# A decoder layer on one core: squares of the next group's input further behind their loads, priority for masked values and for heads' second parts, the last group's first two output blocks stored singly

## The chip, the cores and the metric

The kernel runs on one core of a Trainium2 chip. A core has four compute engines that run their own instruction streams, TensorE (PE, matrix products, with its weight load PEld beside it), VectorE (DVE), ScalarE (ACT) and GpSimd (POOL), and SyncE (SP), which here issues nearly all of the transfers (DMA) between the chip's memory and the core's own. The streams wait for each other by semaphores. The metric is the device time of one launch in microseconds (us); smaller is better.

## The reference

One layer of a decoder, in fp32, for a prompt of 2048 tokens and for 8 samples of 8 tokens that share the weights (model width 1024):

```python
hp = rmsnorm(x, norm_mix_w)
proj = hp @ w_in                       # 8 parts of 4 heads x 128
rq, rk, rv, rg, hq, hf, hi, hg = split(proj)
# 4 RetNet heads: rotary q and k, decay 1 - 2^(-5-h), state S <- g*S + k^T v, o = q S
# 4 HGRN2 heads: f = lb + (1-lb)*sigmoid(hf), state S <- diag(f) S + (1-f)^T hi, o = silu(hq) S
o = head_rmsnorm(o) * silu(gate)       # per head
x = x + concat(o) @ w_out
x = x + square(relu(rmsnorm(x) @ w_up)) @ w_down
y = rmsnorm(x)                         # and the heads' final states, of prompt and samples
```

## The kernel before, in words

**Numbers and tiles.** Tokens lie in the free dimension, 128 features in the partitions. A product of fp32 operands is made from "first parts" (`hi`, rounded to fp32r by a copy) and "second parts" (`lo`, the remainder, one subtraction): hi*hi, hi*lo and lo*hi, three matmuls into one PSUM tile. For weights, `hi` is L311 on ACT and `lo` L318 on DVE; for the groups' input the pair is L1961 (ACT) and L1965 (DVE), named `first` and `second` of `halve`, and "cut" in `operands`. The larger products are made from quarters of their operands in seven products instead of eight, which needs sums of quarters: L429 and L1901 for weights (kept in the chip's memory for later groups: L436 stores the sums, L400 the first and second parts), L879 (`total`) for the input.

**The work in stages.** The tokens come in three groups: group 0 has the 64 sample tokens and 512 of the prompt (T = 576), groups 1 and 2 have 768 each. For each group `mix` goes through four head pairs (p = 0 to 3): it projects queries, keys and gates (products L464 in group 0, L1125 and L1868 later), the values (L1202, L1206 in group 0), and runs the chunks of the retention and of the gated recurrence: scores L1482, turns of keys L1393, states and outputs L1707, L1709, L1715, samples L1324, L1327, L1378. The heads' outputs go to memory (L1241) until the group's heads are complete, are loaded back (L1236), transposed on PE and cut (`cut_heads`, L1857 to L1859). `out_proj` projects them in 8 blocks, in two loops in group 0: the first three heads' part first, evicted onto the residual, then the last head's. Then the MLP runs for the group, and the next group begins.

**Early operands.** While group 0's last head and output projection run, group 1's input is already read and prepared by `norm_blocks` with `early`: `operands` loads four quarters of x (`load`, L1941 on SP), squares them for the RMSNorm (`square`: L854 on ACT, the sum L856 on DVE), multiplies them by the norm's weight (`weigh`, L863 on ACT, two instructions each), cuts them, and makes the sums L879 and cuts these. It does so for v = 0 and for v = 1; the squares' sum then goes through L2038, L682, L683 and PE's column sums L688 and L689 to the factor of the norm. Group 2's input is prepared in the same way during group 1's MLP, without squares.

**What sets the order.** The program is written along PE's steps. `later(ticks, fn)` puts a step on an agenda so many ticks (steps of PE's products) ahead, and it is emitted when that tick comes. The instructions so emitted get their place on each engine from a scheduler, which estimates when each is ready; `soon` (L246) emits an instruction with high priority, and an instruction so emitted is listed under L246 in a profile, whatever it does; `keep_in_program_order` pins it against others so marked. DMA issues have a place in SP's or ACT's order like any instruction, so a transfer that waits holds up those behind it.

**The places that the change touches.** `sample_blocks` (L1366) multiplies a value tile by the samples' mask for `sample_update` (L1378 on PE, L1382 and L1385 on DVE). `cut_heads` makes the first part of the transposed heads on ACT and the second on DVE:

```python
self.tc.keep_in_program_order(nc.scalar.activation(hi[:, a:e], ps, AF.Copy, scale=w))
nc.vector.scalar_tensor_tensor(out=lo[:, a:e], in0=ps, scalar=w, in1=hi.bitcast(F32)[:, a:e], ...
```

`finish_last` ends the program: the last group's column sums (L2427 on PE), the norm's factor (L2358 and L2359 on ACT), eight multiplies L2436 of 128 partitions x 384 on DVE, each half of the columns of a pair of blocks, and four stores L2437, one for each pair (`np_` 0 to 3), alternately issued by SP and ACT.

## Time and profile before

| | |
|---|---|
| median of 3 runs | 2358.68 us (2358.43 to 2358.98) |
| the profiled execution | 2359.45 us |
| its span (first to last instruction) | 2357.6 us |
| PE busy | 2337.3 us (99%) |
| DVE busy | 1792.8 us (76%) |
| ACT busy | 1227.3 us (52%) |
| POOL busy | 139.1 us (6%) |
| chain of work that ended last | PE 93%, DVE 3%, ACT 1%, DMA 1%, issue 1% |
| moved by DMA | 575.60 MB, mean 244 GB/s |

Busy is the time in which an engine works on an instruction; issuing transfers and waiting on semaphores are not counted. The chain is followed back from the last instruction, at each step to what released it. Profile rows of several instructions give their count as x4; the releaser in brackets ("0.72 <-ACT slab L246") is the idle time before the row and what ended it. Names without numbers (slab, ld, raw, pj, mm) are pools of buffers: slab and ld are 128 x 768 tiles, ld those that transfers fill; pj and mm lie in PSUM, which PE writes.

### The profile page before, as it was taken

What the parts mean: (1) busy time and instruction counts of PE and PEld (TensorE: products, weight loads), DVE (VectorE), ACT (ScalarE), POOL (GpSimd) and SP (SyncE); (2) the same over time, 40 slices, a digit from 0 to 9 for tenths busy, and PEclk for the clock granted to TensorE, in tenths of its full rate; (3) what the DMA queues carried; (4) which work ended last, traced back from release to release, by engine and by line L of the source; (5) the groups of instructions that cost most, each with busy time, mean ns of one, the idle gap of its engine ahead of it and who ended that gap; (6) DMA issues with size and microseconds to landing.
All of it is one profiled execution on the core that took longest, in us unless ns stands there. A gap on an engine that the chain in (4) does not pass through costs nothing.

```text
span 2357.6 us, 39360 instructions
## 1 busy us (share of the span) xinstructions
PE 2337.3 (99%) x15340; PEld 2301.6 (98%) x15340; DVE 1792.8 (76%) x2309; ACT 1227.3 (52%) x1976; POOL 139.1 (6%) x199
## 2 busy tenths in 40 slices
PE   9999999999999999999999999999999999999998
PEld 8888899999999999999999999999999999999997
DVE  8766766777666776668769988666988787669887
ACT  5556555557645555546455546444544364445443
POOL 3221201111001100100000000000000000000000
PEclk9999999999999999999999999999999999999999
DMA  9888887779866777898677665767665458675642
GB/s 317 285 296 298 267 314 255 280 266 324 302 226 242 273 285 286 300 344 304 219 258 262 219 219 189 248 206 229 224 194 186 152 192 270 194 232 179 207 154 70
DMA packets 232649, 575.60 MB, mean 244 GB/s; under 512 B 24195, under 2 KB 92803, under 8 KB 232454
## 3 DMA queue, kind: packets, MB, share of 16 engines
q1 hardware_dynamic: 231766, 572.20, 71.3%
q8 instruction: 122, 2.00, 0.4%
q10 hardware_dynamic: 688, 0.80, 0.1%
q14 instruction: 73, 0.60, 0.1%
HBM read 419.95 MB, written 151.66 MB: 242 GB/s over the span
## 4 chain that ended last, share of the span: by engine, by line
PE 93%; DVE 3%; ACT 1%; DMA 1%; issue 1%; POOL 0%; SPq 0%; DVEq 0%; POOLq 0%; ACTq 0%
PE pj L1868 36%; PE pf L1868 28%; PE pj L464 11%; PE pj L1125 10%; PE pj L1206 2%; PE mm L1707 1%; PE mm L1715 1%; PE mm L1709 1%; PE mm L1393 1%; PE mm L1482 1%; PE mm L1635 1%; PE mm L1206 0%; PE mm L1857 0%; DVE raw L429 0%; DVE lo L318 0%
## 5 line engine op out<-in xcount | busy, mean ns | idle before, releaser
L1868 PE MATMUL pj<-slab,hi 128*128 128x384 f32 (+1 forms) x3504 | 853.4, 326 | 0.0
L311 ACT CAST hi<-raw 128x1024 fp32r<-128x1024 f32 x446 | 468.6, 1051 | 692.1 <-PE pj L1868 264.6
L318 DVE TENSOR_TENSOR lo<-raw,hi 128x1024 fp32r<-128x1024 f32 x446 | 545.8, 1224 | 157.3 <-ACT hi L311 152.2
L1868 PE MATMUL pf<-slab,hi 128*128 128x384 f32 (+1 forms) x2768 | 652.2, 321 | 0.0
L1868 PEld LDWEIGHTS pj<-slab,hi 128*128 128x128 f32 x3504 | 614.3, 188 | 0.0
L1868 PE MATMUL pj<-slab,lo 128*128 128x384 f32 (+1 forms) x1752 | 570.7, 326 | 0.0
L1868 PEld LDWEIGHTS pf<-slab,hi 128*128 128x128 f32 x2768 | 480.0, 188 | 0.1
L1868 PE MATMUL pf<-slab,lo 128*128 128x384 f32 (+1 forms) x1384 | 443.1, 320 | 0.0
L1868 PEld LDWEIGHTS pj<-slab,lo 128*128 128x128 f32 x1752 | 329.3, 188 | 0.0
L1125 PE MATMUL pj<-hi,slab 128*128 128x256 f32 x1344 | 260.4, 287 | 0.3 <-DVE slab L246 0.3
L1868 PEld LDWEIGHTS pf<-slab,lo 128*128 128x128 f32 x1384 | 260.1, 188 | 0.0
L464 PE MATMUL pj<-slab,hi 128*128 128x288 f32 (+1 forms) x1216 | 243.4, 316 | 2.1 <-ACT slab L246 1.0
L1125 PEld LDWEIGHTS pj<-hi,slab 128*128 128x128 f32 x1344 | 214.9, 191 | 0.6 <-DVE slab L246 0.6
L464 PEld LDWEIGHTS pj<-slab,hi 128*128 128x128 f32 x1216 | 194.2, 188 | 5.3 <-issue 1.8
L1125 PE MATMUL pj<-lo,slab 128*128 128x256 f32 x672 | 190.1, 283 | 0.0
L1961 ACT CAST slab<-slab 128x768 fp32r<-128x768 f32 (+1 forms) x192 | 145.4, 779 | 62.9 <-DVE slab L1972 47.4
L246 DVE TENSOR_TENSOR slab<-pj,slab 128x768 f32<-128x768 f32 (+2 forms) x136 | 124.2, 915 | 70.4 <-PE pj L1868 27.3
L1965 DVE TENSOR_TENSOR slab<-slab 128x768 fp32r<-128x768 f32 (+1 forms) x192 | 167.3, 886 | 13.2 <-ACT slab L1961 4.6
L464 PE MATMUL pj<-slab,lo 128*128 128x288 f32 (+1 forms) x608 | 143.5, 315 | 0.0
L1125 PEld LDWEIGHTS pj<-lo,slab 128*128 128x128 f32 x672 | 128.7, 192 | 0.0
L464 PEld LDWEIGHTS pj<-slab,lo 128*128 128x128 f32 x608 | 102.6, 188 | 0.3 <-issue 0.2
L2217 DVE TENSOR_TENSOR slab<-pf,slab 128x768 f32<-128x768 f32 (+1 forms) x87 | 76.5, 884 | 24.4 <-PE pf L1868 24.2
(265 smaller groups left out, 2572.0 us busy)
## 6 DMA issues: line engine op xcount, KB each, us to landing
raw<-w SPq DMA_DIRECT2D x254, 512.0 KB, 5.2
slab<-fu SPq DMA_DIRECT2D x64, 384.0 KB, 5.3
fu<-ld SPq DMA_DIRECT2D x60, 384.0 KB, 3.9
ld<-fin SPq DMA_DIRECT2D x28, 384.0 KB, 5.0
ld<-x SPq DMA_DIRECT2D x24, 384.0 KB, 7.0
slab<-fu SPq DMA_DIRECT2D x32, 288.0 KB, 4.8
fu<-ld SPq DMA_DIRECT2D x30, 288.0 KB, 3.2
slab<-x SPq DMA_DIRECT2D x16, 384.0 KB, 6.7
```

The source lines that it names most:

```text
L246: return fn(*a, **k)
L311: self.nc.scalar.copy(self.wts[j][0], raw)
L318: self.nc.vector.tensor_tensor(out=lo, in0=raw, in1=hi.bitcast(F32), op=ALU.subtract)
L464: self.nc.tensor.matmul(pj[:, i, :T2], w, a[:, c0:c1], start=j == 0 and q == 0, stop=j == n - 1 and q == 2)
L1125: self.nc.tensor.matmul(ps[:, tb * 256:(tb + 1) * 256], t, w[:, cols], start=first and kb == j == 0 and tb != 1, stop=kb == KB // 2 - 1 an ...
L1206: nc.tensor.matmul(dst, t[:, s:s + C], ww, start=kb == 0 and q == 0, stop=last and q == 2, skip_group_check=True)
L1393: nc.tensor.transpose(ps[:, j * P:(j + 1) * P], src[:, c], self.ident)
L1482: nc.tensor.matmul(ps[:, j * P:(j + 1) * P], k[:, cols[c]], q[:, cols[c]], start=True, stop=True)
L1868: m = self.nc.tensor.matmul(*a, **k)
L1961: self.nc.scalar.copy(hi[:, :g.T], B[name][:, :g.T])
L1965: self.nc.vector.tensor_tensor(out=lo[:, :g.T], in0=B[name][:, :g.T], in1=hi.bitcast(F32)[:, :g.T], op=ALU.subtract)
L2217: nc.vector.tensor_tensor(out=r, in0=ps, in1=r, op=ALU.add)
```

## The change

It alters the ticks of three calls and of three steps in `operands`, the priority of two DVE instructions, and the end:

- group 1's early operands: v = 0 loads from tick 40 instead of 44 and sums from 92 instead of 88; v = 1 from 96 and 148 instead of 100 and 144;
- in `operands`, each quarter's square comes 22 ticks behind its load instead of 9, its weighing 24 instead of 12 (20 where there are no squares), its cut 30 instead of 18 (26);
- the masked values and the heads' second parts are emitted with `soon`;
- of the last group's four output pairs the first is multiplied block by block (four multiplies of 128 x 192, in program order) and stored as two blocks, one by SP and one by ACT; the other three pairs stay pairs, and go to SP, ACT, SP where they went to ACT, SP, ACT.

```diff
--- before.py
+++ after.py
@@ -830,7 +830,7 @@
 
         if early:
             x.update(split=split, factor=factor, factor_t=factor_t)
-            self.operands(g, 0, 44, 88, x, 186)
+            self.operands(g, 0, 40, 92, x, 186)
             return
         todo = [(m, v, h) for h in range(2) for m in range(2) for v in range(2)]
         for k, a in enumerate(todo):
@@ -870,10 +870,10 @@
             t = t0 + 7 * j
             self.later(t, load, name)
             if sums is not None:
-                self.later(t + 9, square, name)
-            self.later(t + (12 if sums is not None else 20), weigh, name)
+                self.later(t + 22, square, name)
+            self.later(t + 24, weigh, name)
             if name != "B12":
-                cut(t + (18 if sums is not None else 26), name)
+                cut(t + 30, name)
         def total(name, into):
             a, op, b = T_SUMS[name]
             nc.vector.tensor_tensor(out=B[into][:, :g.T], in0=B[a][:, :g.T], in1=B[b][:, :g.T], op=op)
@@ -904,7 +904,7 @@
             self.later(164, tables)
             self.later(176, rotary)
             return
-        self.operands(g, 1, 100, 144, g.x)
+        self.operands(g, 1, 96, 148, g.x)
         for h in range(2):
             self.later(146 + 4 * h, g.x["split"], h)
             self.later(154 + 4 * h, g.x["factor"], h)
@@ -1363,7 +1363,7 @@
         for i in range(2):
             vm = self.getr()
             v = w[i].bitcast(F32)[:96, which * P:(which + 1) * P]
-            self.nc.vector.tensor_tensor(out=vm[:96, :512].rearrange("p (s v) -> p s v", v=P),
+            self.soon(self.nc.vector.tensor_tensor, out=vm[:96, :512].rearrange("p (s v) -> p s v", v=P),
                                          in0=v.unsqueeze(1).to_broadcast([96, 4, P]),
                                          in1=self.con[:96, C_SM:C_SM + 4].unsqueeze(2).to_broadcast([96, 4, P]), op=ALU.mult)
             out.append(vm)
@@ -1856,8 +1856,8 @@
                     c = (j - j0) * 256 + hd * P
                     nc.tensor.transpose(ps[:, s:s + n], o[:n, c:c + P], self.ident[:n, :n])
                 self.tc.keep_in_program_order(nc.scalar.activation(hi[:, a:e], ps, AF.Copy, scale=w))
-                nc.vector.scalar_tensor_tensor(out=lo[:, a:e], in0=ps, scalar=w, in1=hi.bitcast(F32)[:, a:e],
-                                               op0=ALU.mult, op1=ALU.subtract)
+                self.soon(nc.vector.scalar_tensor_tensor, out=lo[:, a:e], in0=ps, scalar=w, in1=hi.bitcast(F32)[:, a:e],
+                          op0=ALU.mult, op1=ALU.subtract)
             g.oc[p].append((hi, lo))
 
     def pair(self, g, slab):
@@ -2430,11 +2430,18 @@
             t = self.get()
             for ps, c in zip(x["ps"], two):
                 self.soon(self.last_factor, ps, t[:, c])
-            for np_ in range(4):
+            y = self.outputs(g, 0)
+            for c in two:
+                for i in range(2):
+                    r = block(i)[:, c]
+                    self.tc.keep_in_program_order(nc.vector.tensor_tensor(out=r, in0=r, in1=t[:, c], op=ALU.mult))
+            for i, queue in enumerate((nc.sync, nc.scalar)):
+                queue.dma_start(y[:, i], block(i))
+            for np_ in range(1, 4):
                 r = self.pair(g, g.R[np_ % 2][np_ // 2, 0])
                 for c in two:
                     nc.vector.tensor_tensor(out=r[:, :, c], in0=r[:, :, c], in1=t[:, c].unsqueeze(1).to_broadcast([P, 2, w // 2]), op=ALU.mult)
-                (nc.scalar if np_ % 2 else nc.sync).dma_start(self.outputs(g, 0)[:, 2 * np_:2 * np_ + 2], r)
+                (nc.sync if np_ % 2 else nc.scalar).dma_start(y[:, 2 * np_:2 * np_ + 2], r)
 
         for d, fn, *a in ((13, squares), (14, weigh, 0), (15, weigh, 1), (17, total), (19, square, 2), (20, third), (21, weigh, 2),
                           (25, square, 3), (26, lambda: sums(x["sum"], True)), (27, weigh, 3), (29, lambda: sums(x[3], False)), (30, outs)):
```

How this moves instructions is seen in three places. All rows are in the order in which the engine runs them; a row of several equal instructions has their count behind it.

The first place is group 0's last head. On DVE, from the first sum of squares on, there stood before:

```order
L856 TENSOR_TENSOR slab<-slab 128x768
L1965 TENSOR_TENSOR slab<-ld,slab 128x768
L246 TENSOR_TENSOR slab<-pj,ld 128x576
L1755 SCALAR_TENSOR_TENSOR slab<-mm,rs,slab 128x128 x2
L1965 TENSOR_TENSOR slab<-ld,slab 128x768
L1755 SCALAR_TENSOR_TENSOR slab<-mm,rs,slab 128x128 x2
L856 TENSOR_TENSOR slab<-slab 128x768
L1965 TENSOR_TENSOR slab<-ld,slab 128x768
L1022 TENSOR_TENSOR slab<-slab 128x576
L318 TENSOR_TENSOR lo<-raw,hi 128x1024
```

and now:

```order
L856 TENSOR_TENSOR slab<-slab 128x768
L246 TENSOR_TENSOR slab<-pj,ld 128x576
L1755 SCALAR_TENSOR_TENSOR slab<-mm,rs,slab 128x128 x4
L1965 TENSOR_TENSOR slab<-ld,slab 128x768
L1022 TENSOR_TENSOR slab<-slab 128x576
L318 TENSOR_TENSOR lo<-raw,hi 128x1024
L1965 TENSOR_TENSOR slab<-ld,slab 128x768
L318 TENSOR_TENSOR lo<-raw,hi 128x1024
```

The second part of the value weights (L318) has two cuts and the second sum of squares less ahead of it. On SP, a little later, the heads' results (fo) are loaded back; before:

```order
L1241 DMA fo_2851<-slab 128x512
L252 DMA raw<-w 128x1024 x3
L1236 DMA ld<-fo_1336 128x768
L1236 DMA ld<-fo_1338 128x512
L1236 DMA ld<-fo_2068 128x768
L1236 DMA ld<-fo_2070 128x512
L436 DMA fsi3VS_2898<-raw 128x2x256
L1236 DMA ld<-fo_2849 128x768
L436 DMA fsi3VS_2905<-raw 128x2x256
```

and now:

```order
L1241 DMA fo_2847<-slab 128x512
L252 DMA raw<-w 128x1024 x2
L436 DMA fsi3VS_2898<-raw 128x2x256
L436 DMA fsi3VS_2905<-raw 128x2x256
L400 DMA fki3VA11hi<-hi 128x2x256
L1236 DMA ld<-fo_1336 128x768
L1236 DMA ld<-fo_1338 128x512
L400 DMA fki3VA11lo<-lo 128x2x256
L252 DMA raw<-w 128x1024
L1236 DMA ld<-fo_2068 128x768
L1236 DMA ld<-fo_2070 128x512
```

Three stores of 256 KB stand ahead of the first load now, and a store and a weight load of 512 KB between the first two loads and the next two.

The second place is the end of the same head's values on PE, with the turns L1393 of its keys. pj tiles are numbered as allocated; mm_3057 and mm_3084 are the turns' tiles. Before:

```order
L1206 MATMUL pj_2799<-hi_2878,slab_176 128x512
L1206 MATMUL pj_2799<-lo_2879,slab_176 128x512
L1206 MATMUL pj_2799<-hi_2878,slab_177 128x512
L1206 MATMUL pj_2799<-hi_2878,slab_184 128x512
L1206 MATMUL pj_2799<-lo_2879,slab_184 128x512
L1393 MATMUL mm_3057<-con_78,slab_2413 128x128 x2
L1206 MATMUL pj_2799<-hi_2878,slab_185 128x512
L1627 MATMUL mm_3062<-slab_2711,slab_2795 128x64
L1393 MATMUL mm_3084<-con_78,slab_2413 128x128 x2
L1206 MATMUL pj_2798<-hi_2878,slab_176 128x512
```

and now:

```order
L1206 MATMUL pj_2797<-hi_2878,slab_176 128x512
L1393 MATMUL mm_3057<-con_78,slab_2413 128x128 x2
L1206 MATMUL pj_2797<-lo_2879,slab_176 128x512
L1206 MATMUL pj_2797<-hi_2878,slab_177 128x512
L1627 MATMUL mm_3062<-slab_2703,slab_2793 128x64
L1393 MATMUL mm_3084<-con_78,slab_2413 128x128 x2
L1206 MATMUL pj_2797<-hi_2878,slab_184 128x512
L1206 MATMUL pj_2797<-lo_2879,slab_184 128x512
L1206 MATMUL pj_2797<-hi_2878,slab_185 128x512
L1206 MATMUL pj_2796<-hi_2878,slab_176 128x512
```

Both turns stand three or four products earlier.

The third place is the output projection of group 0 on DVE, where the first loop's last block is evicted (from pj_3715, block 8) and the second loop's first (from pj_3786, in the new order pj_3775). Before:

```order
L2038 TENSOR_TENSOR slab_2597<-slab_2597 128x384
L1965 TENSOR_TENSOR slab_3747<-ld_3691,slab_3746 128x768
L246 TENSOR_TENSOR slab_3265<-pj_3786,slab_3265 128x576
L246 TENSOR_TENSOR slab_3778<-pj_3715,slab_3713 128x576
L856 TENSOR_TENSOR slab_2685<-slab_2685,slab_3764 128x768
```

and now:

```order
L2038 TENSOR_TENSOR slab_2652<-slab_2652 128x384
L246 TENSOR_TENSOR slab_3767<-pj_3715,slab_3713 128x576
L1965 TENSOR_TENSOR slab_3765<-ld_3683,slab_3764 128x768
L246 TENSOR_TENSOR slab_3265<-pj_3775,slab_3265 128x576
L856 TENSOR_TENSOR slab_2724<-slab_2724,slab_3791 128x768
```

Block 8's eviction now stands ahead of the cut and of the next block's eviction.

## Rows read from the trace of the kernel before

**Rows 1.** The page: busy time of PE, its share of the span, its instructions.

```profile
PE 2337.3 (99%) x15340; PEld 2301.6 (98%) x15340; DVE 1792.8 (76%) x2309; ACT 1227.3 (52%) x1976; POOL 139.1 (6%) x199
```

**Rows 2.** Windows of 50 us: length, each engine's busy us, clock, DMA share, GB/s.

```profile
200.00:250.00 50.00, 47.78 (x318) 41.70 (x314) 42.44 (x71) 33.95 (x76) 15.36 (x16) 1.00 0.80 269
250.00:300.00 50.00, 47.57 (x348) 42.27 (x348) 35.55 (x69) 29.72 (x78) 6.89 (x11) 1.00 0.91 303
300.00:350.00 50.00, 49.15 (x335) 48.85 (x335) 35.93 (x45) 31.99 (x48) 1.93 (x3) 1.00 0.87 309
...
550.00:600.00 50.00, 48.77 (x349) 47.24 (x348) 44.83 (x73) 33.43 (x71) 7.04 (x9) 1.00 0.87 299
```

**Rows 3.** Waits of PE: us in total, times, longest.

```profile
PE mm L1709 <- ACT slab L246: 1.1, 1, 1.1
...
PE pj L464 <- ACT slab L246: 1.0, 1, 1.0
PE pj L464 <- DVE slab L246: 0.9, 1, 0.9
PE pj L1202 <- DVE lo L318: 0.8, 1, 0.8
PE mm L1378 <- DVE slab L1366: 0.7, 1, 0.7
PE pj L1206 <- ACT slab L246: 0.7, 1, 0.7
PE mm L1857 <- DVE slab L1859: 0.5, 1, 0.5
```

**Rows 4.** Timeline of PE, 233 to 235 us: start, length, instruction, idle before.

```profile
233.19 0.39 PE L1202 MATMUL pj<-hi,slab 128*128 128x512 f32 x1
233.42 0.39 PE L1206 MATMUL mm<-hi,slab 128*128 128x512 f32 x1
234.65 0.50 PE L1202 MATMUL pj<-lo,slab 128*128 128x512 f32 x1 [0.85 <-DVE lo L318]
```

**Rows 5.** Timeline of ACT, 219 to 221 us.

```profile
219.74 0.84 ACT L854 ACTIVATE slab<-ld 128x768 f32<-128x768 f32 x1 [1.53 <-DMA ld<-x]
220.49 0.39 ACT L246 ACTIVATE slab<-S,G 128x128 f32<-128x128 f32 x1
```

**Rows 6.** Timeline of DVE, 230 to 233 us.

```profile
230.96 0.96 DVE L856 TENSOR_TENSOR slab<-slab 128x768 f32<-128x768 f32 x1
231.84 0.95 DVE L1965 TENSOR_TENSOR slab<-ld,slab 128x768 fp32r<-128x768 f32 x1
```

**Rows 7.** Timelines of POOL, SP (issues) and PE, 237 to 245 us.

```profile
237.72 2.77 POOL L1021 TENSOR_TENSOR slab<-slab,ld 128x576 f32<-128x576 f32 x1 [8.20 <-ACT slab L246]
...
240.52 0.80 SPq L1236 DMA_DIRECT2D ld<-fo  x2
...
244.40 0.86 PE L1857 MATMUL mm<-con,ld 64*128 64x64 f32 x5
```

**Rows 8.** Lines L1021 (all), L1236 issued at 241.0, L1236 (all): ns; us to landing.

```profile
L1021 POOL TENSOR_TENSOR slab<-slab,ld x8: 1429/1442/2772, 32.2 to 237.7; 128x576 f32<-128x576 f32 x8
...
DMA to landing us min/median/max: 3.2/3.2/3.2
...
DMA to landing us min/median/max: 2.8/4.4/9.2
```

**Rows 9.** Timeline of ACT, 259 to 264 us.

```profile
259.33 0.37 ACT L1395 COPY slab<-mm 128x256 f32<-128x256 f32 x1 [1.14 <-PE mm L1393]
...
262.88 1.05 ACT L311 CAST hi<-raw 128x1024 fp32r<-128x1024 f32 x1 [1.20 <-DMA fki3VA22hi<-hi]
```

**Rows 10.** Timeline of DVE, 316 to 320 us.

```profile
318.78 1.42 DVE L246 TENSOR_TENSOR slab<-pj,slab 128x576 f32<-128x576 f32 x2 [1.90 <-PE pj L464]
```

**Rows 11.** Timeline of DVE, 2346 to 2352 us.

```profile
2346.80 3.84 DVE L2436 TENSOR_TENSOR slab<-slab 128x384 f32<-128x384 f32 x8 [0.72 <-ACT slab L2359]
```

**Rows 12.** Line L2437, the last stores: us from issue to landing.

```profile
DMA to landing us min/median/max: 3.6/5.2/5.2
```

## The prediction

> **What bounds the kernel now.** Read the engines' busy times first: TensorE (PE) works 2337.3 us of a 2357.6 us span, 99% [rows 1]. A change that adds no arithmetic can therefore pay only where PE stands idle. The table of 50 us stretches shows where that is: PE has 47.78, 47.57 and 49.15 us of 50 in the three stretches from 200 to 350 us, and 48.77 from 550 to 600 [rows 2]: 6.7 us are missing in these four together. The list of PE's waits then says for whom it stood idle [rows 3]: six of the seven entries lie between 219 and 320 us, that is in the last head (p = 3) of the first group and in its output projection, where the change moves squares, loads and second parts. The seven make 5.7 us; the start and the tail have what else PE lacks. A wait costs PE a restart on top: after the 0.8 us for L1202 the matmul starts 1.23 us after the one before, where two neighbours stand 0.23 apart [rows 4], 1.0 in all. I count 0.2 for each restart.
>
> The sum is made against the profiled execution, 2359.45 us (its span of 2357.6 and 1.85 around it); it lies 0.77 above the median of 2358.68. 0.2%, about what a measurement of this kernel can tell from no change, is 4.7 us.
>
> **The parts, in the order of time.**
>
> *First square (PE waits at 219.4).* PE waits 1.1 us for ScalarE's (ACT's) next state, L246 [rows 3]. ACT stood idle 1.53 us for a load of x, squared it for 0.84 us, and only then reached L246 at 220.49 [rows 5]. Moving the squares 13 ticks behind their loads is just what should remove this. But in the new order the first L854 still stands ahead of that L246, and the loads' issue stands at the same place on SP, behind the two stores of the samples' states. So I take 0. Bounds: a gain of 1.3, the whole wait with its restart, or a loss of 1.5, ACT's idle time once more, if the load lands that much later now that a second one follows it at once on SP.
>
> *Second part of the value weights (PE waits at 233.4).* PE waits 0.8 us for L318 on VectorE (DVE) [rows 3]. An L856 at 230.96 and an L1965 at 231.84, of the squares and the cuts, stood ahead of it [rows 6]. Both now stand behind it: L318 starts twice 0.88 us earlier, and the wait goes, 1.0 us with its restart.
>
> *But the next wait is close.* PE comes to the heads' first transposes (L1857) at 244.40, without a wait [rows 7]. They read head results that SP loads back at L1236, first issued at 240.52, when GpSimd (POOL) ends its L1021 (237.72 plus 2.77) and with it the last use of the buffer; the second load lands 3.2 us after its issue at about 241.0 [rows 7, 8], so at 244.2. PE would now come 1.0 us earlier, and by the new order the transposes stand three products (0.7 us) sooner: it would be there at 242.7. ACT's copy that starts L1021 keeps its time in the new order, because it stands behind a cut that needs a DVE sum. So most of the 1.0 is waited away again. Net gain between 1.0 (loads earlier) and -0.5 (three stores of 256 KB now go out ahead of them): I take 0.4.
>
> L1021's own length decides here: seven of the eight took about 1.44 us, this one 2.77, beside DVE operations that read two SBUF tensors [rows 8]. The Trainium skill, "SBUF — State Buffer", section "Who interferes with whom", says that a DVE instruction with two SBUF inputs and a GpSimd instruction that reads SBUF exclude each other, and whichever issues second waits until the first is done. The long row agrees with it, and DVE still has such instructions at that time in the new order, so by that rule the length is a matter of which came first.
>
> *Masked values and second parts of the heads get priority.* PE waited 0.7 us for L1366 at 282.5 [rows 3]; there the order of DVE is unchanged (two L965, L1382, L1965 still ahead): 0. For heads 1 and 2 it does change, but their masked values are not among PE's waits: 0. The heads' second parts (L1859) now go ahead of the weight sums L429 around 249 us; of what PE lacks from 200 to 250 [rows 2] the named waits leave 0.3, so this gives between 0 and 0.3, and I take 0.2.
>
> *Evictions of the last values (PE waits at 259.9).* PE waits 0.7 us for ACT's L246 [rows 3]; ACT had itself been idle 1.14 us for the turn L1393, until 259.33 [rows 9]. In the new order that turn stands four products earlier, so the evictions can run beside them. Gain 0 (if the turn's PSUM buffer is not free sooner) to 0.9 with the restart: 0.6.
>
> *First out-projection blocks (PE waits at 263.5).* PE waits 1.0 us for L246 on ACT [rows 3], which stands behind an L311 that waited 1.20 us, until 262.88, for the store of kept weights fki3VA22hi [rows 9]. That store stood on SP behind stores of weight sums; three of the sums (L429) now come ahead of an L246 and the scans L1437 on DVE, and SP is past them sooner. Gain 0 to 1.2: 0.8.
>
> *The eighth block (PE waits at 318.5).* PE waits 0.9 us for DVE [rows 3]: DVE, idle 1.90 us for PE, first evicts block 1 of the second loop and then block 8 of the first [rows 10], so the next block finds no free buffer. In the new order block 8 comes three places earlier, ahead of an L1965, in that idle time. Gain 1.1, or 0 if block 8's x, whose load now stands one transfer later on SP, is not there yet; DVE's idle time leaves 1.9 us for that: 0.8.
>
> *Group 1's first head (590 us).* PE waits 0.5 us for L1859 [rows 3], and again for the L246 behind it. Now all four L1859 go ahead of L246, and all twelve transposes ahead of the products. The fourth L1859 lengthens L246's wait by about 0.5 us, of which the three transposes that PE does meanwhile fill 0.3: a loss of 0.2 (0 to 0.5). The same swap in group 2's head and group 2's later sums lie in stretches without a gap: 0.
>
> *The end.* Eight multiplies take 3.84 us together, 0.48 each [rows 11]; two of them become four halves. Halves cost between half and all of a whole, so the last store goes 0 to 0.96 us later; I take 0.2, near the lower end, since an operation on so many elements is mostly its elements. The first store gets out hardly earlier, because a pair's multiply stands between the halves. As the stores land 3.6 to 5.2 us after their issue [rows 12], being queued behind each other, the smaller first stores may give 0.4 back. I take a loss of 0.1 (-0.4 to 0.9). The Trainium skill, "DMA: Bandwidth & Descriptors", section "Issuing engines are not separate DMA queues", says that transfers from different engines run on the same 16 DMA engines and interleave, and that using several only saves issue time; that speaks against any gain from splitting the pair over SP and ACT, and the landing times of 5.2 us agree.
>
> **Sum.** Gains 0.4 + 0.2 + 0.6 + 0.8 + 0.8 = 2.8, losses 0.2 + 0.1 = 0.3: 2.5 us. The profiled execution would take 2356.95, the median 2358.68 - 2.5 = **2356.2 us**.
>
> **Rivals.**
> - *The gaps only move.* PE arrives earlier at the transposes, at fki3VA22hi's landing and at the x loads, and waits there instead. For it: [rows 7, 9] show both limited by transfers that PE does not drive. Against: block 8's eviction is a plain matter of order. Gains of 0 to 1, losses as above: about 2358.5.
> - *The loads of the heads come 1.3 us earlier*, because L1021 takes 1.44 us as its seven siblings did [rows 8]: the whole 1.0 at 233.4 stays, 0.6 more than summed: 2355.6. The rule of the page "SBUF — State Buffer" would allow it.
> - *All gaps close*, the first square's too, with every term at its upper end: 1.3 + 1.0 + 0.3 + 0.9 + 1.2 + 1.1 = 5.8, less 0.3: 2353.2. Against it: the order at 219.4.
> - *The loads of the heads come late, and the kernel is slower.* They now stand on SP among sums' stores and weight loads, two of them behind a 512 KB load. The slowest L1236 took 9.2 us to land where the one at 241.0 took 3.2 [rows 8]: 6.0 us of idle PE, of which the later gaps up to 264 (0.2 + 0.9 + 1.2) are absorbed and 0.8 comes back at 318.5: 2.9 us, with the losses 3.2 slower, 2361.9. It decides from a landing about 3 us later than now. Two such loads would cost over 4.7.
> - *The change doesn't do what it says*: seen already for head 3's masked values and the first square, whose orders stand; it is in the sum as two zeros.
>
> **How the numbers follow.** The forecast 0.46, gaps only moving 0.26, early head loads 0.11, all gaps 0.09, late head loads 0.08. The predicted time is the first. Faster by over 0.2% (under 2354.0) needs the case of all gaps: 0.09. Slower by over 0.2% needs two late loads: 0.04. Within: 0.87. The range runs from 2353.5, where all terms are near their upper ends, to 2360.5, halfway into the late loads; outside it are the last of these and most of the case of all gaps.
>
> **What would show it.** PE's list of waits would keep L1709 <- L246 (about 1.1) and L1378 (0.7), lose L1202 <- L318 and L464 <- DVE L246, and gain an entry L1857 <- DMA of up to 1 us. ACT's L311 would no longer wait for fki3VA22hi; PE busy in 200 to 250 should be 47.8 to 48.4, in 250 to 300 above 48.5, in 300 to 350 near 49.9. At 590 the two waits would be one. The prediction is wrong if the square no longer stands before L246, if a load holds PE for more than 2 us, or if the tail behind the last matmul changes by over 0.5 us.

## The result, and the profile after

The kernel became slower: **2363.32 us** in the median of 20 runs (2359.84 to 2366.94), where the kernel before took 2358.18 in 20 runs beside it (2356.98 to 2359.22). The ratio is 1.0021, with a 95% interval of 1.0015 to 1.0027. That is 5.1 us, just over what the prediction called measurable, and on the other side of the forecast. The changed kernel's times also spread over 7 us, where those of the kernel before spread over 2. On a second chip it stood at 1.0016 (1.0007 to 1.0025).

| | before | after |
|---|---|---|
| profiled execution, its span | 2359.45, 2357.6 | 2361.83, 2359.9 |
| PE busy | 2337.3 | 2338.3 |
| last matmul's end to the end of the span | 11.2 | 10.9 |

The profiled execution lies below the changed kernel's median, so it shows 2.4 us of the loss. The windows answer to [rows 2], with one more at 950 us; the columns are the same.

```profile
200.00:250.00 50.00, 47.06 (x316) 41.44 (x314) 41.60 (x70) 34.89 (x77) 14.14 (x16) 1.00 0.87 292
250.00:300.00 50.00, 48.61 (x358) 43.75 (x359) 37.03 (x73) 29.35 (x78) 7.03 (x11) 1.00 0.91 303
300.00:350.00 50.00, 47.68 (x316) 47.36 (x315) 33.98 (x41) 30.78 (x45) 0.01 (x1) 0.97 0.85 302
550.00:600.00 50.00, 48.75 (x343) 47.02 (x342) 44.61 (x73) 34.61 (x75) 7.26 (x10) 1.00 0.87 302
950.00:1000.00 50.00, 49.62 (x380) 49.45 (x379) 30.60 (x52) 25.54 (x68) 2.51 (x3) 1.00 0.86 307
```

From 250 to 300 PE gained 1.0 us. But from 300 to 350 it lost 1.5, and there the granted clock is 0.97, where every window of [rows 2] has 1.00. The waits of PE answer to [rows 3]:

```profile
PE pj L1868 <- ACT slab L246: 2.3, 1, 2.3
PE mm L1857 <- DVE slab L246: 2.0, 2, 1.5
PE mm L1709 <- ACT slab L246: 1.8, 1, 1.8
...
PE mm L1378 <- DVE slab L246: 0.9, 2, 0.7
PE pj L1125 <- DVE slab L246: 0.7, 2, 0.4
PE pj L1206 <- ACT slab L246: 0.5, 1, 0.5
```

Four waits of before are gone as forecast: the one at 233, both for out-projection blocks (263 and 318), and the one at 260. (The 0.5 us for L1206 is another one, at 122 us.) The first line is new, and so is the 1.5 us in the second; the other 0.5 there is the old wait for L1859, which is listed under L246 now that `soon` emits it. L1709's has grown from 1.1 to 1.8.

**The wait of 2.3 us.** It lies at 337 us, in the first products of group 1 (L1868). ACT's timeline of the changed kernel there:

```profile
333.95 1.05 ACT L311 CAST hi<-raw 128x1024 fp32r<-128x1024 f32 x1
334.89 0.77 ACT L1931 ACTIVATE slab<-slab,vec 128x576 f32<-128x576 f32 x1
335.57 0.82 ACT L1961 CAST slab<-ld 128x768 fp32r<-128x768 f32 x1
337.69 1.04 ACT L311 CAST hi<-raw 128x1024 fp32r<-128x1024 f32 x1 [1.29 <-PE pj L1868]
338.64 0.77 ACT L1931 ACTIVATE slab<-slab,vec 128x576 f32<-128x576 f32 x1
339.32 1.49 ACT L246 COPY slab<-pj 128x768 f32<-128x768 f32 x2
```

The COPY (L1048 in the program, recorded as L246) evicts the first product, and the third product needs its PSUM bank. It stands behind an L311 that rounds weights for a later product and is itself waiting 1.29 us for PE to be done with a buffer of the second. So PE finishes the second product, and stands still until rounding, L1931 and COPY are through. In the kernel before the COPY came first:

```profile
338.84 0.77 ACT L246 COPY slab<-pj 128x768 f32<-128x768 f32 x1
339.52 1.05 ACT L311 CAST hi<-raw 128x1024 fp32r<-128x1024 f32 x1
```

There it ended at 339.61. The third product began at 340.01, without a wait, behind the 48 matmuls of the first two (from 331.51 on) and one other:

```profile
340.01 0.51 PE L1868 MATMUL pj<-slab,hi 128*128 128x384 f32 x2
```

So the COPY was in time by 0.4 us. What follows the wait in the changed kernel, in PE's timeline:

```profile
337.49 0.34 PE L1868 MATMUL pj<-slab,lo 128*128 128x384 f32 x1
340.15 0.62 PE L1868 MATMUL pj<-slab,hi 128*128 128x384 f32 x2 [2.32 <-ACT slab L246]
...
342.05 0.52 PE L1868 MATMUL pj<-slab,lo 128*128 128x384 f32 x1
342.37 0.84 PE L1868 MATMUL pj<-slab,hi 128*128 128x384 f32 x2
```

And in its windows of 2 us, where the third number from the end is PE's granted clock:

```profile
338.00:340.00 2.00, 0.00 (x0) 0.00 (x0) 2.00 (x3) 2.00 (x4) 0.00 (x0) 1.00 0.64 167
340.00:342.00 2.00, 1.85 (x8) 1.85 (x9) 0.66 (x1) 0.80 (x2) 0.00 (x0) 0.80 0.79 242
342.00:344.00 2.00, 2.00 (x8) 2.00 (x8) 0.00 (x0) 0.00 (x0) 0.00 (x0) 0.50 0.91 342
344.00:346.00 2.00, 2.00 (x11) 2.00 (x10) 0.00 (x0) 0.00 (x0) 0.00 (x0) 0.84 1.03 390
```

After the still stretch the clock falls to 0.50, that is 1.2 in place of 2.4 GHz, and the matmuls start 0.32 us apart in place of 0.174: eleven of them, 1.6 us. With the wait and its restart (2.48 from start to start, above the usual distance) this place costs 4.1 us. Until there the change had won: group 1's first product starts at 329.34, 2.17 us earlier than before.

**The wait of 1.5 us.** It lies at 249 us, where PE's L1857 needs the heads' second parts. The chain to it begins on POOL, whose small rows (L1443 to L1450) make G; ACT's L1456 waits for it, with all of the head's work behind it. POOL's timeline of the changed kernel:

```profile
241.92 0.75 POOL L1443 COPY ends<-slab 128x4 f32<-128x4 f32 x1 [2.16 <-DVE slab L1437]
242.64 0.92 POOL L1444 TENSOR_TENSOR ends<-slab 128x4 f32<-128x4 f32 x1
243.63 0.59 POOL L1450 TENSOR_TENSOR G<-ends 128x4 f32<-128x4 f32 x1
```

And ACT's:

```profile
244.25 0.20 ACT L1456 ACTIVATE G<-G 128x4 f32<-128x4 f32 x1 [5.28 <-POOL G L1450]
244.37 1.03 ACT L311 CAST hi<-raw 128x1024 fp32r<-128x1024 f32 x1
245.30 0.83 ACT L1961 CAST slab<-ld 128x768 fp32r<-128x768 f32 x1
...
246.81 0.69 ACT L1455 ACTIVATE slab<-slab 128x576 f32<-128x576 f32 x1
```

POOL was hardly later than before: L1456 ran at 244.11 there. What is new is a row on each of two engines. In the kernel before the L1961 (the cut, which DVE's L1965 needs) ran at 239.24 already, ahead of this wait. Moved behind its load, it now stands after it and ahead of L1455, which ran at 245.93 before. On DVE, where L1466 waits for L1455, an L318 of 1.33 us now stands between L1466 and the second parts (L246). DVE's timeline of the changed kernel:

```profile
247.53 0.76 DVE L1466 TENSOR_TENSOR slab<-slab 128x576 f32<-128x576 f32 x1 [0.41 <-ACT slab L1455]
...
248.88 1.33 DVE L318 TENSOR_TENSOR lo<-raw,hi 128x1024 fp32r<-128x1024 f32 x1
250.13 1.39 DVE L246 SCALAR_TENSOR_TENSOR slab<-mm,vec,slab 128x320 fp32r<-128x320 f32 x3
```

And of the kernel before, where the second parts are L1859:

```profile
247.16 0.74 DVE L1466 TENSOR_TENSOR slab<-slab 128x576 f32<-128x576 f32 x1
...
249.21 0.54 DVE L1859 SCALAR_TENSOR_TENSOR slab<-mm,vec,slab 128x320 fp32r<-128x320 f32 x1
```

So the second parts come 0.9 us later, at a PE that is ahead of its old time.

### The profile page after: what moved, and what is told of

Same layout as the page of the kernel before. It is cut to its first block, busy times and chain, and to the rows that moved or that the text cites. A ratio compares the mean times of both kernels' runs of the same rounds, so it can differ in the third digit from the quotient of the medians.

```text
span 2359.9 us, 39359 instructions
## 1 busy us (share of the span) xinstructions
PE 2338.3 (99%) x15340; PEld 2304.1 (98%) x15340; DVE 1792.2 (76%) x2311; ACT 1227.8 (52%) x1976; POOL 140.6 (6%) x199
## 4 chain that ended last, share of the span: by engine, by line
PE 93%; DVE 3%; ACT 2%; issue 1%; DMA 1%; POOL 1%; SPq 0%; DVEq 0%; POOLq 0%; ACTq 0%
PE pj L1868 36%; PE pf L1868 28%; PE pj L464 11%; PE pj L1125 9%; PE pj L1206 2%; PE mm L1707 1%; PE mm L1715 1%; PE mm L1709 1%; DVE slab L246 1%; PE mm L1393 1%; PE mm L1482 1%; PE mm L1635 1%; PE mm L1206 1%; PE mm L1857 1%; DMA raw<-w 1%
## 5 line engine op out<-in xcount | busy, mean ns | idle before, releaser
L1868 PE MATMUL pj<-slab,hi 128*128 128x384 f32 (+1 forms) x3504 | 854.5, 327 | 2.3 <-ACT slab L246 2.3
L311 ACT CAST hi<-raw 128x1024 fp32r<-128x1024 f32 x446 | 468.8, 1051 | 691.2 <-PE pj L1868 270.5
L318 DVE TENSOR_TENSOR lo<-raw,hi 128x1024 fp32r<-128x1024 f32 x446 | 546.4, 1225 | 156.4 <-ACT hi L311 148.1
L1868 PE MATMUL pf<-slab,hi 128*128 128x384 f32 (+1 forms) x2768 | 652.3, 321 | 0.0
L1868 PEld LDWEIGHTS pj<-slab,hi 128*128 128x128 f32 x3504 | 615.5, 188 | 2.6 <-ACT slab L246 2.6
L1868 PE MATMUL pj<-slab,lo 128*128 128x384 f32 (+1 forms) x1752 | 571.4, 326 | 0.0
L1868 PEld LDWEIGHTS pf<-slab,hi 128*128 128x128 f32 x2768 | 480.3, 188 | 0.1
L1868 PE MATMUL pf<-slab,lo 128*128 128x384 f32 (+1 forms) x1384 | 443.1, 320 | 0.0
L1868 PEld LDWEIGHTS pj<-slab,lo 128*128 128x128 f32 x1752 | 329.8, 188 | 0.0
L1125 PE MATMUL pj<-hi,slab 128*128 128x256 f32 x1344 | 260.2, 287 | 0.7 <-DVE slab L246 0.7
L1868 PEld LDWEIGHTS pf<-slab,lo 128*128 128x128 f32 x1384 | 260.1, 188 | 0.0
L1125 PEld LDWEIGHTS pj<-hi,slab 128*128 128x128 f32 x1344 | 214.8, 191 | 1.1 <-DVE slab L246 0.6
L1125 PE MATMUL pj<-lo,slab 128*128 128x256 f32 x672 | 190.1, 283 | 0.0
L1961 ACT CAST slab<-slab 128x768 fp32r<-128x768 f32 (+1 forms) x192 | 145.4, 779 | 63.9 <-DVE slab L1972 47.4
L246 DVE TENSOR_TENSOR slab<-pj,slab 128x768 f32<-128x768 f32 (+2 forms) x136 | 124.3, 915 | 71.1 <-PE pj L464 24.6
L1965 DVE TENSOR_TENSOR slab<-slab 128x768 fp32r<-128x768 f32 (+1 forms) x192 | 167.3, 886 | 13.0 <-ACT slab L1961 4.4
L1125 PEld LDWEIGHTS pj<-lo,slab 128*128 128x128 f32 x672 | 128.7, 192 | 0.0
```

The lines of the kernel that those rows point to most:

```text
L246: return fn(*a, **k)
L311: self.nc.scalar.copy(self.wts[j][0], raw)
L318: self.nc.vector.tensor_tensor(out=lo, in0=raw, in1=hi.bitcast(F32), op=ALU.subtract)
L1125: self.nc.tensor.matmul(ps[:, tb * 256:(tb + 1) * 256], t, w[:, cols], start=first and kb == j == 0 and tb != 1, stop=kb == KB // 2 - 1 an ...
L1868: m = self.nc.tensor.matmul(*a, **k)
L1961: self.nc.scalar.copy(hi[:, :g.T], B[name][:, :g.T])
```

## The experiments

All were compared with the kernel before on the same chip. The theory from the traces (A) is the order at 337; its rivals are that the clock falls anyway (B), and that the priority for the heads' second parts costs it all (C).

**One row of ACT moved.** Two rows are pinned behind all that the program issued before them on ACT; in the traces no other row of any engine moves against the changed kernel.

```diff
-            self.nc.scalar.copy(self.wts[j][0], raw)
+            (self.tc.keep_in_program_order if self.fast and j in (44,) else (lambda i: i))(self.nc.scalar.copy(self.wts[j][0], raw))
...
-            self.soon(nc.scalar.copy, b2(t), ps)
+            (self.tc.keep_in_program_order if self.fast and self.w_next in (43,) else (lambda i: i))(self.soon(nc.scalar.copy, b2(t), ps))
```

> The changed kernel with one row of ScalarE moved: the eviction of group 1's first product (COPY, L246) is held ahead of the rounding of the S3 sum's weights (L311), which stands in front of it in the changed kernel. Theory A (that order costs the 2.5 us wait of TensorE at 337 us and the stretch of half clock behind it): the wait at 337 goes, the granted clock from 340 to 346 is 0.98 or more, and the time is 2358.2 - 1.9 (the lead that the profile of the changed kernel has at 330 us) + 0.5 (its wait at 952 us) - 0.3 (end) = 2356.5, between 2355.5 and 2358. Theory B (the clock falls because the work runs closer together, with that wait or without it): the wait goes but a stretch at a clock under 0.9 stays between 300 and 350, time 2360 to 2361. Theory C (the loss is the priority for the heads' second parts): time within 0.5 of the changed kernel's 2363.3.

Measured: 2360.18 us, ratio 1.0009 (1.0000 to 1.0018), 1.8 above the kernel before. The window of the trace:

```profile
300.00:350.00 50.00, 50.00 (x342) 49.24 (x341) 36.66 (x46) 33.08 (x49) 0.94 (x2) 1.00 0.91 319
```

Wait and low clock are both gone there, so A holds for that place. B falls by the trace alone, since 2360.18 lies in its range; C falls by the time. But the time was 2.2 us above A's range. The profiled execution, the slowest of the eleven (2362.95), shows a wait at 249 that had grown to 3.4 us. The growth is on POOL; the timeline of this run:

```profile
243.09 3.76 POOL L1443 COPY ends<-slab 128x4 f32<-128x4 f32 x1 [2.16 <-DVE slab L1437]
246.81 0.20 POOL L1444 TENSOR_TENSOR ends<-slab 128x4 f32<-128x4 f32 x1
```

DVE's timeline beside it:

```profile
246.12 0.68 DVE L429 TENSOR_TENSOR raw<-raw 128x512 f32<-128x512 f32 x1
249.23 0.96 DVE L1965 TENSOR_TENSOR slab<-ld,slab 128x768 fp32r<-128x768 f32 x1 [2.44 <-ACT slab L1961]
```

The same COPY of 128x4 elements that took 0.75 us took 3.76, and ended at 246.85, just when DVE's unbroken work ended (246.80). The rows behind it, with DVE idle, took 0.20 each, where the changed kernel's took 0.92 and 0.59 beside a busy DVE. Of the eleven times four lie from 2362.16 up and seven from 2360.85 down, which would fit a row of 3.76 us in some executions and of 0.75 in the others; one profile does not show it.

**The operands' new numbers alone** (the lines of `operands` and its two calls from the diff, nothing else).

> The kernel before with the numbers of the operands alone changed (squares, weighings, splits and starts), nothing else. Theory A: ScalarE has the changed kernel's order at 335 to 340 us, so the wait of about 2.5 us at 337 and the half clock are there; the waits on the heads' second parts (1.4 us more at 249, 0.5 at 952) are not: 2363.3 - 1.9 + 0.3 (end as before) = 2361.7, between 2360 and 2363. Theory B: the same time, with the low clock. Theory C: no loss is left and the forecast's gains stay, 2356 to 2357.

Measured: 2362.22 us, 1.0016 (1.0007 to 1.0026), 3.9 above. A wait of 2.5 us from start to start at 339 and a low clock behind it (0.59 and 0.56 in the two windows from 342 to 346), as A expected; but the wait at 249 is there as well (3.5 from start to start, L1443 again 3.76), so it doesn't come from the heads' priority. The row in PE's timeline:

```profile
252.11 0.44 PE L1857 MATMUL mm<-con,ld 128*128 128x128 f32 x2 [3.37 <-DVE slab L1859]
```

**The rest of the change alone** (both priorities and the end's stores).

> The kernel before with the two priorities and the end's stores, without the operands' new numbers. Theory A: ScalarE has the order of before at 338 us, so no wait there over 0.3 us; what is left is the price of the heads' second parts (up to 1.4 at 249, 0.1 at 592, 0.5 at 952) less 0.3 at the end: 2358.2 to 2359.9. Theory B: as before, 2358. Theory C: the whole loss, 2361 to 2363.

Measured: 2361.30 us, 1.0013 (1.0004 to 1.0022): more than A expected (1.4 us above its range), with nothing at 337. The trace has a new place, at 259 us, which a later run explains.

**The row moved, and no priority for the heads' second parts.**

```diff
-                self.soon(nc.vector.scalar_tensor_tensor, out=lo[:, a:e], in0=ps, scalar=w, in1=hi.bitcast(F32)[:, a:e],
+                nc.vector.scalar_tensor_tensor(out=lo[:, a:e], in0=ps, scalar=w, in1=hi.bitcast(F32)[:, a:e],
...
```

> As the run with the one row moved, and the heads' second parts (L1859) without their priority. Theory A: 2356.5 less what that priority costs at 249 and 952 us: 2354.7, between 2353.5 and 2356.5, with no wait of L1857 over 0.3 us at 249. If the wait of 1.6 us at 249 stays, the priority was not its cause and the time is that of the run with the row moved alone. Theory B: 2358 to 2359.

Measured: 2359.86 us, 1.0006 (0.9997 to 1.0015). The wait at 249 stays (1.44 from start to start): A's reading of it was wrong, and the new one (D) was that POOL sets it; its rival (E) is the order of ACT's and DVE's own rows. The next four runs were on another chip.

**The chunk ends on VectorE.** The row moved, and in `reaches`:

```diff
-            lf, bb, dd = x["lf"], self.get(), self.get()
+            lf, bb, dd, small = x["lf"], self.get(), self.get(), nc.vector if self.fast and n0 and p == 3 else nc.gpsimd
...
-            nc.gpsimd.tensor_copy(e[:, p, E_MID + c0:E_MID + c0 + n], mid)
+            small.tensor_copy(e[:, p, E_MID + c0:E_MID + c0 + n], mid)
```

(and the three others likewise).

> The changed kernel with the one row of ScalarE moved, and in group 0's last head pair the four small operations of the chunk ends (L1443, L1444, L1448, L1450) on VectorE in place of GpSimd. Theory D (what is left of the loss is the wait of L1857 at 249 us, and it begins on GpSimd, whose L1443 took 0.75 us in two of the profiles and 3.76 us in two others, while VectorE had work without a break; ScalarE's L1456 waits for it with all of the head's evictions behind it): the wait at 249 falls under 0.3 us and the time by 1.6 to 3.5 against the run with the row moved alone: 2360.2 - 2.6 = 2357.6, between 2356.3 and 2358.8. Theory E (that wait is made by the order of ScalarE's and VectorE's own rows, rounding and L318 ahead of the evictions): a wait of 1.2 or more stays, 2359 to 2360.5.

Measured: 2358.31 us, 1.0000 (0.9991 to 1.0009), no longer slower than before. The wait of L1857 at 249 is 0.3 us, 0.46 from start to start:

```profile
250.72 0.44 PE L1857 MATMUL mm<-con,ld 128*128 128x128 f32 x2 [0.30 <-DVE slab L246]
```

That is D, at the edge of its "under 0.3"; and 0.7 us more turn up at 281 and 1.5 at 629. E falls in the form it had: in this trace the L311 and the L318 still stand where E put the cause. But D is shown only so far: the chain starts earlier without POOL's rows, and the wait goes. In the profiles with L1443 at 0.75 the rows L1961 and L318 have a part in it, as shown above, and taking them out of the way alone was not tried.

**The same without the heads' priority.**

> The same, and the heads' second parts (L1859) without their priority. Theory D: another 0.5 us less, the wait at 952: 2357.1, between 2355.8 and 2358.3, faster than the kernel before by 1. Theory E: 2359 to 2360, as with the row moved and no priority.

Measured: 2356.68 us, 0.9995 (0.9986 to 1.0004); 1.7 below the kernel before. Its profile was of its slowest run and shows the next thing in line: group 1's L863 waits for a load of x, with the next state (L246) behind it.

```profile
629.16 0.61 ACT L863 ACTIVATE ld<-ld,vec 128x384 f32<-128x384 f32 x1 [3.05 <-DMA ld<-x]
629.68 0.39 ACT L246 ACTIVATE slab<-S,G 128x128 f32<-128x128 f32 x1
```

**The chunk ends alone, in the kernel before.**

> The kernel before with these four small operations on VectorE, nothing else. In its profile the wait at 249 is 0.23 us, so theory D expects 0.2 or less gained: 2358.2, between 2357.3 and 2359. If the kernel before loses on GpSimd in some runs too, its highest times go and the median falls by 0.5 or more.

Measured: 2358.95 us, 1.0001 (0.9992 to 1.0010): nothing, as D expected. Where the operands' numbers are the old ones (before, and the runs of the rest of the change and its parts), every profile with that row on POOL has it at 0.75.

**The changed kernel again.**

> The changed kernel once more, on the chip of these runs, for its time beside the others and for a second profile. Theories A and D: 2362 to 2364; in the profile the wait at 337 of 2.5 us with 1.6 or more of half clock behind it, and at 249 a wait of either about 1.6 or about 3.5 us, according to whether L1443 took 0.75 or 3.76 us. A profile with neither, at the same time, would speak against both.

Measured: 2361.44 us, 1.0016, 0.6 under the expected range. The waits are the same, 2.5 and 1.6 from start to start at 337 and 249 (L1443 at 0.75). But the low clock is not there, in its fastest run (2360.39); the windows of 2 us after the wait:

```profile
340.00:342.00 2.00, 1.74 (x10) 1.74 (x11) 0.77 (x1) 0.91 (x2) 0.00 (x0) 1.00 0.86 254
342.00:344.00 2.00, 2.00 (x13) 2.00 (x12) 0.00 (x0) 0.00 (x0) 0.00 (x0) 1.00 0.97 334
```

So the low clock is not part of every execution. Low clock or not, and L1443 at 0.75 or 3.76, are two reasons for the changed kernel's wide spread; that they explain all of it is argued, not shown. On this chip, then, the changed kernel stands at 2361.44, with the two repairs at 2358.31, and without the heads' priority as well at 2356.68.

The next three were on a third chip. **The next state ahead of the square**, on top of the last version without the heads' priority:

```diff
-            self.soon(nc.scalar.activation, x["St"][:, c * P:(c + 1) * P], self.S[:, H + p], AF.Copy, scale=x["G"][:, c:c + 1])
+            self.ns = self.soon(nc.scalar.activation, x["St"][:, c * P:(c + 1) * P], self.S[:, H + p], AF.Copy, scale=x["G"][:, c:c + 1])
...
-            nc.scalar.activation(y[:, :g.T], B[name][:, :g.T], AF.Square)
+            with self.tc.issue_after(self.ns.ins) if self.fast and not v and g.i == 1 and name == 'B11' else __import__('contextlib').nullcontext(): nc.scalar.activation(y[:, :g.T], B[name][:, :g.T], AF.Square)
```

> As the run with the row moved, the chunk ends on VectorE and no priority for the heads' second parts; and besides, the first square of group 1 (L854) is held behind the eviction-like row that makes group 0's next state (L246, slab from S and G), which TensorE's L1709 waits for at 219 us. Theory F (a row of ScalarE that needs nothing stands behind one that waits for a transfer, the same fault as at 337): the wait of 2.0 us at 219 to 220 falls under 0.4 and the time from 2356.7 to 2355, between 2354 and 2356.5, faster than the kernel before. Rival G (TensorE, earlier by 2 us, meets the next late transfer or row at 232 to 282 or at 628 us): the wait goes and comes back there, and the time stays between 2356.3 and 2358.

Measured: 2357.94 us, 0.9999 (0.9990 to 1.0008). That is rival G's range. The profile is of one of the slower executions (2361.05): the L246 now runs at 219.29, and the wait at 219 is gone; but PE waits 1.5 us at 237 for DVE, and 0.7 twice from 262 to 265, with a clock of 0.50 behind those (266 to 268).

**The heads' priority alone.**

> The kernel before with the priority for the heads' second parts alone. Theory F: ScalarE has the rounding L311, which waits for a transfer, ahead of the evictions L1395 and L246 at 259 us (it does so in the order of its rows, and did in the run of the priorities and the end together), so TensorE waits 2.5 us there in place of 1.1, and the time is that of that run, 2360 to 2362. Theory H (that run's loss came from the masked values or the end's stores): 2358 to 2359.

Measured: 2359.79 us, 1.0010 (1.0001 to 1.0019), a touch under the expected range. ACT's timeline shows the fault of 337 in another place: a rounding that waits for a store, ahead of the evictions that PE waits for.

```profile
259.13 1.04 ACT L311 CAST hi<-raw 128x1024 fp32r<-128x1024 f32 x1 [1.45 <-DMA fki3VA22hi<-hi]
260.08 0.36 ACT L1395 COPY slab<-mm 128x256 f32<-128x256 f32 x1
```

In [rows 9] the L1395 ran at 259.33 and the L311 at 262.88, behind it. PE waits 2.2 us here, and the clock falls to 0.50 in the window from 262 to 264.

**Masked values and the end alone.**

> The kernel before with the priority for the masked values and the end's single stores alone. Theory F: no row of ScalarE moves near a wait of TensorE: 2358.1, between 2357.3 and 2358.8 (0.3 less at the end). Theory H: 2360 to 2362.

Measured: 2358.01 us, 0.9999 (0.9990 to 1.0008): nothing, as expected.

Two last runs ask what the forecast's gain is worth once the faults are mended. **The new numbers alone, with both repairs:**

> The operands' new numbers alone (no priorities, the end's stores as before), with the two repairs: the one row of ScalarE moved at 337 us, and the chunk ends on VectorE. If the forecast's gains (the waits at 233, 260, 263 and 318 us) are real and the two faults were all that took them back, it stands as the run with the same repairs and no heads' priority, 0.3 above it at the end: 2357.0, between 2356 and 2358, under the kernel before by about 1. If the masked values' priority or the stores made that run fast, 2358 to 2359.

Measured: 2357.16 us, 0.9996 (0.9987 to 1.0005), 0.7 below. One of its twelve executions took 4678.94 us and is left out of the ratio. It was the profiled one, and its page shows the same 15340 matmuls at twice the busy time, with DVE and ACT hardly changed against [rows 1]:

```profile
PE 4665.3 (100%) x15340; PEld 4166.5 (89%) x15340; DVE 1811.6 (39%) x2313; ACT 1240.1 (27%) x1976; POOL 126.7 (3%) x195
```

So PE worked at half its pace from start to end, though the windows of that trace give a granted clock of 1.00; why is open. At that pace hardly a wait is left, so whether the repairs removed those at 249 and 337 in this run has no trace.

**The fastest version again:**

> The fastest version so far (row moved, chunk ends on VectorE, no priority for the heads' second parts) on another chip, beside the kernel before: 2356.0 to 2357.5 and under the kernel before by 1 to 2 if the first set of 11 times was no accident; 2358 or more if it was.

Measured: 2357.00 us, 0.9996 (0.9987 to 1.0005), 0.8 below, between 2356.10 and 2357.52. Its windows:

```profile
200.00:250.00 50.00, 47.53 (x318) 41.81 (x313) 42.92 (x77) 34.74 (x78) 11.36 (x12) 1.00 0.85 291
250.00:300.00 50.00, 48.20 (x355) 43.25 (x355) 36.59 (x70) 29.32 (x78) 7.19 (x11) 1.00 0.91 300
300.00:350.00 50.00, 50.00 (x339) 49.78 (x338) 34.89 (x42) 31.35 (x45) 3.46 (x3) 1.00 0.89 322
```

It stood below the kernel before on both chips it ran on, by 1.7 and 0.8 us. Neither interval excludes no change, so a gain of about 1 us is likely and not shown.

## Why the prediction was wrong

*The sum's first terms held.* By the distance from one matmul's start to the next, above the usual one of its shape: the second part at 233 cost 1.0 and costs nothing (forecast 1.0). The evictions at 260 and the turn ahead of them cost 1.1 together, and now 0.1 (forecast a gain of 0.6). The out-projection blocks cost 1.15 and 1.0, and now nothing (0.8 and 0.8). Group 1's first head lost 0.1 (0.2). The end gained 0.3 (forecast a loss of 0.1), inside its bounds, and every profile with the new end has it: 10.9 to 11.0 us behind the last matmul, against 11.1 to 11.2. A half took 0.35 us where a whole takes 0.48 [rows 11], so the gain should lie in the stores, which was not tried apart. The first square, taken at 0, lost 0.65, inside its bounds: its load landed later, and the L246 stood behind it as forecast.

*"But the next wait is close: 0.4."* A wait did take the place of the one at 233, but not there and not for that reason. PE came to the first transposes at 243.46 and no L1236 held it, since L1021 took 1.42 us this time, as the rival at 0.11 had it. PE was held at the next L1857, at 249, by the chain behind POOL's L1450 with the new rows in it: 1.4 us more than before in this profile and 3.3 in two others. Net of the 1.0 at 233 this term is -0.4 to -2.3, not +0.4. The prediction did weigh a long POOL row against DVE's work, yet only for L1021; in the two others the row that grew was L1443.

*"The same swap in group 2's head lies in a stretch without a gap: 0."* It made one: 0.5 us at 952, where L1125 waits for DVE.

*The step that failed: the sum ended at 320 us.* It counted what each removed wait gave, and let PE carry the 2.5 us to the end, as though nothing were due behind it. Of its 2.8 up to there 2.2 arrived at 329 (0.2 of them were there at 219 already, ahead of the first wait that it counted). But ACT's eviction, in time by 0.4 us in the kernel before, was the next limit, and the new order put a waiting L311 ahead of it: 4.1 us lost where 49.9 us of work in 300 to 350 was forecast and 47.68 came. The order of ACT's rows at that place was to be seen beforehand, and the text read ACT's order only where PE waited already. The rivals had waits that take a removed one's place, but on transfers.

*The chances.* The one slower rival was a late transfer at 0.08; slower by a row of an in-order engine had no chance at all, though the text itself explained four of the seven waits [rows 3] by rows that stand in an engine's order, those at 219, 233, 263 and 318. The heads' priority, taken as a gain of 0.2, costs 1.7 us alone; in the changed kernel, with the new numbers, the loss at 259 does not show, and taking the priority out there gained 1.6 us beside the two repairs and 0.3 beside the first alone, neither clear of the noise.

## What to carry to other kernels

When a change removes waits, follow the engine that gains to the next buffer it needs, and look how late that buffer comes free now: here a margin of 0.4 us stood against a gain of 2.2. On an engine that works in order, a row that waits for a transfer or a buffer should not stand ahead of one that empties a PSUM bank. Ticks and priorities did not keep that order here, at 337 and at 259 us; at 337 pinning the two rows did. (That the scheduler took the rounding as ready is likely and was not looked at.) Watch a small operation between two engines on a critical chain: here a COPY of 128x4 took 0.75 or 3.76 us on POOL beside a busy DVE, and 0.16 on DVE itself.

## What was not expected of the hardware

- A COPY of 128x4 elements on POOL took 0.75 us in seven profiles and 3.76 in two, with the same work on DVE beside it (in three of the seven in the same order), and 0.2 was enough for the next rows, of 128x4 and 128x8, once DVE was idle. The Trainium skill, "SBUF — State Buffer", section "Who interferes with whom", has it that the two engines lock each other out for a whole instruction, by order of issue. The trace of the changed kernel agrees: POOL's row ended at 242.67, 0.05 us after DVE's L1441, beside which it had started. In the first experiment it ended 0.05 us after DVE's last, too, but it had sat out five instructions of DVE, not one, and why it got in between them in other runs no run here shows.
- A wait of 2.3 us was followed by a granted clock of 0.50 in one profile of the changed kernel and by 1.00 in another, at the same place and length; a wait of 3.4 us at 250 in the first experiment was followed by 1.00. At 220 us a wait of 2.0 us was followed by 0.50 in the fourth experiment, and by 1.00 in the fifth. The Trainium skill, "TensorE: Matmul & The Clock Gate", section "What's actually happening", says that the clock is low unless activity raises it and that the point where it changes varies from run to run; the traces agree with the second. The wait at 337 cost 2.5 us in one profile and 4.1 in the other.
